# Seven raw weight slabs and six converted ones, in place of three and eight

## The chip, the cores and the metric

The kernel runs on one core of a Trainium2 chip. The metric is the device time of one execution in microseconds. The core has TensorE (PE, matrix products; weight loads are shown apart as PEld), VectorE (DVE), ScalarE (ACT), GpSimd (POOL) and SyncE (SP), which here issues nearly all the loads, and 16 DMA engines that all queues share.

## The reference

Two layers of a hybrid trunk over 256 tokens of 2048 features, float32. Each layer has a mixer and an MLP, with RMS norms ahead of and behind each:

```
for l in range(2):
    u = rmsnorm(h, g[0])
    proj = u @ w_in[l]                 # layer 0: 2048 x 6144, layer 1: 2048 x 7184
    # layer 0: gated short convolution, and chunked attention with a bias per head
    # layer 1: HGRN2 recurrence, and gated linear attention with a low-rank decay
    y = concat(heads) @ w_out[l]       # 2048 x 2048
    h = h + rmsnorm(y, g[1])
    u = rmsnorm(h, g[2])
    z = square(relu(u @ w1[l])) @ w2[l]    # 2048 x 8192, 8192 x 2048
    h = h + rmsnorm(z, g[3])
```

The weights are read from memory once each, some 400 MB in all.

## The kernel before

The 256 tokens are two tiles of 128 (t = 0 and 1). Every weight matrix is walked in blocks of 512 columns, and each block in slabs: one slab is 256 rows (SLAB = 2 groups of 128) by 512 columns, 512 KB. There are 784 of them.

**A slab's way.** `Block.load` does three things for each slab. SP loads it into a tile `raw` (pool `rawp`, RAW_BUFS buffers). ACT casts it to a high part `whi` in fp32r (L226). DVE subtracts that from the raw slab and so makes the low part `wlo` (L227). `whi` and `wlo` come from the pool `wp`, W_BUFS buffers of each. The raw buffer is free again when the subtraction is done; the pair is free when the last matmul on it is done. Products are made of the parts: high by high, high by low, low by high.

**Two kinds of blocks.** `Block.mm` puts the tokens on the partitions: for each token tile, six matmuls of 512 columns per slab (L240 to L242), with the sum of a block in one PSUM bank `acc`; so one slab is twelve matmuls. `UpBlock.mm` puts the weights' columns on the partitions and takes both token tiles at once: sixteen matmuls per slab, of 512 and 256 columns in turn (L275, L276), into four PSUM banks. At a block's end ACT and DVE empty the banks (`whole` L619, `relu` L453 and L476, and others).

**The order.** `run` (L316) walks the slabs of its blocks: load, hooks, matmuls of both token tiles. Every load of a slab is issued in that order on SP's queue, which also carries the loads of `h`, of `x` and of `norm_g` where a hook puts them. The program text gives priorities; a scheduler fixes, before the run, the order in which each engine gets its instructions, and may put a later matmul that is ready ahead of an earlier one that is not. On the chip each engine works strictly in that order.

**Three special places.** With `tail=4` the last four slabs of a run are walked for token tile 0 first, then for tile 1, so that the norm behind the product can begin for tile 0; the first of the four goes into a buffer of its own (`xhi`, `xlo`). With `lead` (the first run of each MLP) LEAD = 6 slabs are loaded and multiplied for token tile 0, then `lead()` makes the second tile's input (transposes on PE, L185, then `xt` on ACT, L176, and DVE, L178), then the six slabs are multiplied for tile 1. The second mixer begins right behind a run with a tail, so its first slabs too meet a second token tile whose input isn't there yet.

**Other users of raw buffers.** `prep_gla`, `prep_odd` and `load_bias` each take a buffer of `rawp` for a while.

In the second mixer `put_forget` transposes the forget gate `v` on PE, some slabs after its block has ended (`later`); `v` comes out of a chain of exponentials and products on ACT and DVE (L871 to L908).

Of the kernel before, what the change touches and what calls it, by code (L numbers as in the profile page):

```python
# [21 lines left out]
EPS = 1e-6  # L22
NT = 2
SLAB = 2
RAW_BUFS = 3
W_BUFS = 8
LEAD = 6
X_BUFS = 1
ACC_BUFS = 3
# [10 lines left out]
def trunk(ctx, tc, x, norm_g, e_win, rbf, e_wout, o_win, lbraw, smalls, wa2, ba, o_wout, w1, w2,  # L40
# [5 lines left out]
    x2p = ctx.enter_context(tc.tile_pool(name="x2p", bufs=8))  # L46
    rawp = ctx.enter_context(tc.tile_pool(name="rawp", bufs=RAW_BUFS))
    wp = ctx.enter_context(tc.tile_pool(name="wp", bufs=W_BUFS))
    st = ctx.enter_context(tc.tile_pool(name="st", bufs=4))
# [6 lines left out]

    nc.scalar.preload_act_table_set("natural_log_exp_and_others")

# [1 line left out]
    ident = const.tile([P, P], F32, name="ident")  # L60
    nc.scalar.dma_start(out=ident, in_=c_ident)
    ng_rows = const.tile([P, P], F32, name="ng_rows")
# [57 lines left out]
    def gcol(l, i):  # L120
        return ng_t[:, (l * 4 + i) * KT:(l * 4 + i + 1) * KT]

# [1 line left out]
    def rsqrt_of(ss, n, inv, base=None):  # L124
        """(ss * inv + EPS) ** -0.5; with base = (a, b, c, d): (ss * a + c) ** -0.5, where b = -a / 2, d = -c / 2."""
        a, b, c, d = base or (inv, -0.5 * inv, epst, -0.5 * EPS)
        hv = st.tile([P, n], F32, name="rs_v", bufs=4)
        nc.vector.tensor_scalar(out=hv, in0=ss, scalar1=b, scalar2=d, op0=ALU.mult, op1=ALU.add)
        r = st.tile([P, n], F32, name="rs_r", bufs=4)
        nc.scalar.activation(out=r, in_=ss, func=AF.Ln, scale=a, bias=c)  # L130
        nc.scalar.activation(out=r, in_=r, func=AF.Exp, scale=-0.5)
        a = st.tile([P, n], F32, name="rs_a", bufs=4)
        if n == 1:
            nc.vector.scalar_tensor_tensor(out=a, in0=r, scalar=hv, in1=r, op0=ALU.mult, op1=ALU.mult)
        else:
            nc.vector.tensor_tensor(out=a, in0=r, in1=r, op=ALU.mult)
            nc.vector.tensor_tensor(out=a, in0=a, in1=hv, op=ALU.mult)
        o = st.tile([P, n], F32, name="rs_o", bufs=12)
        nc.vector.scalar_tensor_tensor(out=o, in0=a, scalar=1.5, in1=r, op0=ALU.add, op1=ALU.mult)
        return o  # L140

    def powers(r):
        """Factors that stand in for the normalisation ahead of a squared ReLU."""
        r2 = st.tile([P, 1], F32, name="pw2")
        nc.vector.tensor_tensor(out=r2, in0=r, in1=r, op=ALU.mult)
        a, b = [st.tile([P, 1], F32, name="pw4" + n) for n in "ab"]
        nc.vector.tensor_scalar(out=a, in0=r2, scalar1=r2, scalar2=1.0 / D, op0=ALU.mult, op1=ALU.mult)
        nc.vector.tensor_scalar(out=b, in0=a, scalar1=-0.5, scalar2=None, op0=ALU.mult)
        return a, b, r2

    def base_of(ss, pre):
        """What rsqrt_of takes when but the last part of a sum of squares is there."""
        t = total(ss)
        c, d = [st.tile([P, 1], F32, name="base" + n) for n in "cd"]
        nc.vector.tensor_scalar(out=c, in0=t, scalar1=pre[0], scalar2=EPS, op0=ALU.mult, op1=ALU.add)
        nc.vector.tensor_scalar(out=d, in0=c, scalar1=-0.5, scalar2=None, op0=ALU.mult)
        return pre[0], pre[1], c, d

    def total(ss):
        t = st.tile([P, 1], F32, name="rs_t")  # L160
        nc.vector.tensor_reduce(out=t, in_=ss, axis=AX.X, op=ALU.add)
        return t
# [49 lines left out]
    class Block:  # L212
# [6 lines left out]
        def load(self, s, extra=None):  # L219
            k0 = self.kts[s * SLAB]  # L220
            raw = rawp.tile([P, SLAB, 512], F32, name="raw")
            nc.sync.dma_start(out=raw[:, :, 0:self.n], in_=self.wv[:, k0:k0 + SLAB, self.n0:self.n0 + self.n])
            pool, tag, bufs = (wp, "w", W_BUFS) if extra is None else (extra, "x", X_BUFS)
            hi = pool.tile([P, SLAB, 512], F32R, name=tag + "hi", bufs=bufs)
# [29 lines left out]
            return super().get(t, kt)  # L254

    class UpBlock(Block):
        """Columns of the weights on the partitions of the product, both token tiles at once."""

        def __init__(self, wv, n0, n, kts, lhs, evac, banks=None):
            super().__init__(wv, n0, n, kts, lhs, evac)  # L260
# [33 lines left out]
    soon = []  # L294

    def later(f, slabs=2):
        """f() that many slabs from now, so that what it puts on the tensor engine doesn't hold up the products."""
        soon.append([slabs, f])

    def tick(n=1):  # L300
# [50 lines left out]

    ALLK = list(range(KT))

# [1 line left out]
    def sumsq_of(src, jpool):  # L355
        ss = st.tile([P, 4], F32, name="ss4")
        for i in range(4):
            junk = jpool.tile([P, 512], F32, name="junk", bufs=1)
            nc.scalar.activation(out=junk, in_=src[:, i * 512:(i + 1) * 512], func=AF.Square,  # L359
                                 accum_out=ss[:, i:i + 1])  # L360
        return ss
# [27 lines left out]
            return f  # L389
        return t, [load(0), load(1)]  # L390

# [1 line left out]
    def out_proj(l, w, kts, X2, y, h, X, ypool, reload=()):  # L393
        gbc, gl = gbc_tile(ypool, l, 1)
        hooks = {2: gl[0:1], 5: gl[1:2]}
# [95 lines left out]
        run(down(NCH - 1), tail=TAIL, between=finish, extra=ypool)  # L491
        return lambda: finish(1)

# [1 line left out]
    hpool = tc.tile_pool(name="hpool", bufs=1)  # L495
    hp = hpool.__enter__()
    h = [hp.tile([P, D], F32, name=f"h{t}") for t in range(NT)]
# [17 lines left out]
    start = {i: [] for i in range(8)}  # L515
# [34 lines left out]
    yp_cm.__exit__(None, None, None)  # L550
    hpool.__exit__(None, None, None)

# [1 line left out]
    mixpool = tc.tile_pool(name="mix1", bufs=1)  # L554
    mp = mixpool.__enter__()
    X2 = XT()
# [31 lines left out]
def even_mixer(tc, nc, mp, st, aux, x2p, X, X2, rst, w, rbf, sm_t, flip, ident, Block, UpBlock, banks, pair, run,  # L588
# [5 lines left out]
    rbc = {}  # L594

    def spread_norms():
        """The norm factors of the tokens on every partition: as they are, for queries, and squared."""
        ones = mp.tile([P, P], F32, name="ones", bufs=1)
        nc.gpsimd.memset(ones, 1.0)
        ps = aux()  # L600
        for t in range(NT):
            diag = mp.tile([P, P], F32, name="part", bufs=2)
            nc.vector.tensor_scalar(out=diag, in0=ident, scalar1=rst[t], scalar2=None, op0=ALU.mult)
            nc.tensor.matmul(ps[:, t * P:(t + 1) * P], ones, diag, start=True, stop=True)
        for n in ("q", "k", "u"):
            rbc[n] = mp.tile([P, T], F32, name="rbc" + n, bufs=1)
        nc.scalar.copy(out=rbc["k"], in_=ps[:, 0:T])
        nc.scalar.activation(out=rbc["q"], in_=ps[:, 0:T], func=AF.Copy, scale=float(P) ** -0.5)
        nc.vector.tensor_tensor(out=rbc["u"], in0=rbc["k"], in1=rbc["k"], op=ALU.mult)

    def joined(ps, out, scale=None):
        """out = the two parts of a product of UpBlock, times scale."""
        a = mp.tile([P, T], F32, name="part", bufs=2)
        nc.scalar.copy(out=a, in_=ps[:, T:2 * T])
        if scale is None:
            nc.vector.tensor_tensor(out=out, in0=ps[:, 0:T], in1=a, op=ALU.add)
        else:
            z = mp.tile([P, T], F32, name="whole", bufs=2)
            nc.vector.tensor_tensor(out=z, in0=ps[:, 0:T], in1=a, op=ALU.add)  # L619
            nc.vector.tensor_tensor(out=out, in0=z, in1=scale, op=ALU.mult)  # L620
# [124 lines left out]
def odd_mixer(tc, nc, mp, st, aux, x2p, X, X2, rst, w, lbd, prep_gla, sm_t, ident, c_mask,  # L745
# [25 lines left out]
    def heads(a, t):  # L771
        return a.rearrange("p (h t n) -> p h t n", h=4, t=NT)[:, :, t, :]
# [4 lines left out]
    def feature_major(name, pool, bufs):  # L777
        return pool.tile([P, 4 * T], F32, name=name, bufs=bufs)

# [1 line left out]
    def scores(G):  # L781
        """G["K"], G["Q"]: keys and queries, features on the partitions, the queries times their own decay;
        G["B"]: the decay. Level w pairs the first half of each block of 2w tokens with its second half: the keys
        carry the decay up to the end of their half, the queries that from the start of theirs."""
        K, Q, B = G["K"], G["Q"], G["B"]
        sT = mp.tile([P, 8, P], F32, name="sT", bufs=1)
        nc.gpsimd.memset(sT, 0.0)
# [3 lines left out]
        for l, wd in enumerate(LEVELS):  # L791
            ps = aux()
            m = P - wd
            for u in range(8):
# [4 lines left out]
                                 start=True, stop=True)  # L799
            yield  # L800
            nc.vector.copy_predicated(
                out=sT[0:m].rearrange("p u (b two n) -> p u b two n", two=2, n=wd)[:, :, :, 1, :],
# [3 lines left out]
            if wd < 64:  # L806
# [10 lines left out]
                B = nxt  # L817
            else:
                bv = B.rearrange("p (h t two) -> p h t two", h=4, two=2)
                for a, t, i in ((K, 0, 1), (Q, 1, 0)):  # L820
                    half = heads(a, t).rearrange("p h (two n) -> p h two n", two=2)[:, :, 1 - i, :]
# [3 lines left out]
        for hd in range(4):  # L825
            nc.tensor.matmul(ps[:, hd * P:(hd + 1) * P], heads(K, 0)[:, hd, :], heads(Q, 1)[:, hd, :],
                             start=True, stop=True)
# [38 lines left out]
        X2.put(t, kg, split4(x2p, "x2", transpose4(z), sm_t[:, 24 + 4 * kg:28 + 4 * kg]))  # L866

    def neg_sigmoid(x, scale, o=None):
        """-sigmoid(-scale * x): a first reciprocal by exp and ln, then a Newton step."""
        d, r = tmp(), tmp()  # L870
        nc.scalar.activation(out=d, in_=x, func=AF.Exp, scale=scale)  # L871
        nc.vector.tensor_scalar(out=d, in0=d, scalar1=LN_MAX, scalar2=1.0, op0=ALU.min, op1=ALU.add)
        nc.scalar.activation(out=r, in_=d, func=AF.Ln)
        nc.scalar.activation(out=r, in_=r, func=AF.Exp, scale=-1.0)
        nc.vector.tensor_tensor(out=d, in0=d, in1=r, op=ALU.mult)
        o = r if o is None else o
        nc.vector.scalar_tensor_tensor(out=o, in0=d, scalar=2.0, in1=r, op0=ALU.subtract, op1=ALU.mult)
        return o
# [14 lines left out]
        return {"K": feature_major("x2", x2p, None), "Q": feature_major("x2", x2p, None),  # L893
                "B": feature_major("dec", mp, 1), "k": {}, "qk": {}, "v": {0: {}, 1: {}}}

# [1 line left out]
    def hgrn(g):  # L897
        lb = [mp.tile([P, 512], F32, name="gate", bufs=4) for _ in range(2)]
        lsrc = lbd.rearrange("i h d -> i (h d)")
# [34 lines left out]
                Block(wv, HI + g * 512, 512, ALLK, X.get, ev_i),  # L934
                Block(wv, HG + g * 512, 512, ALLK, X.get, ev_g)]

# [1 line left out]
    def gla():  # L938
        G = group()

# [62 lines left out]
    first, decay, rest = gla()  # L1003
# [46 lines left out]
```

## Time and profile before

| what | value |
|---|---|
| median of 3 runs | 2307.85 us (2306.0 to 2311.98) |
| span of the profiled execution | 2302.9 us |
| PE busy | 2276.5 us, 99% |
| PEld busy | 1920.3 us, 83% |
| DVE busy | 1412.6 us, 61% |
| ACT busy | 1093.6 us, 47% |
| DMA, mean over the span | 186 GB/s, the loads of slabs and x 56.2% of 16 engines' span |
| mean granted clock of PE | 0.997 |

The span runs from the first to the last instruction of one profiled execution; the time of a run has a little more around it. A view by time shows for each group of instructions its start, how long it took, its engine, its line in the kernel, what it writes and reads, and in brackets how long its engine stood idle before it and whose work ended that. A cast is ACT's L226, a subtraction DVE's L227.

### The profile page before, as it was taken

How to read it: one execution, taken by the hardware profiler on the slowest of the kernel's cores; microseconds unless marked ns; L12 is line 12 of the kernel's file. 1: busy time of each engine (PE TensorE's matmuls, PEld its weight loads, DVE VectorE, ACT ScalarE, POOL GpSimd, SP SyncE). 2: the span in 40 equal slices, each digit the busy share in tenths (PEclk: the TensorE clock that was granted, in tenths of full speed). 3: DMA queues.
4: the chain of work that ended last, by engine and by line, in shares of the span. 5: the costliest groups of instructions: out<-in, count | busy, mean ns of one | idle time of the engine just before them, and what ended most of it. 6: DMA issues, size and time to landing. Idle time of an engine off the chain costs nothing.

```text
span 2302.9 us, 30049 instructions
## 1 busy us (share of the span) xinstructions
PE 2276.5 (99%) x11518; PEld 1920.3 (83%) x11518; DVE 1412.6 (61%) x1873; ACT 1093.6 (47%) x1565; POOL 15.3 (1%) x30
## 2 busy tenths in 40 slices
PE   9999999999999999999999999999999999999998
PEld 7888888888888888888788888888888888888886
DVE  6656565755555555555777767657656555555555
ACT  6444445544444444444646454546444444444443
POOL 0000000000000000000000000000000000000000
PEclk9999999999999999999999999999999999999999
DMA  7564665655655556555554544565665655655653
GB/s 242 183 187 150 192 205 172 212 189 192 191 186 190 192 187 189 191 190 193 181 193 156 165 146 156 171 243 167 209 193 189 191 190 186 192 192 185 191 192 119
DMA packets 219231, 428.35 MB, mean 186 GB/s; under 512 B 13362, under 2 KB 14160, under 8 KB 218832
## 3 DMA queue, kind: packets, MB, share of 16 engines
q1 hardware_dynamic: 216992, 420.53, 56.2%
q0 software_dynamic: 1376, 4.79, 0.7%
q8 instruction: 90, 1.47, 0.2%
q10 hardware_dynamic: 720, 1.11, 0.1%
q14 instruction: 53, 0.43, 0.1%
HBM read 422.18 MB, written 4.20 MB: 185 GB/s over the span
## 4 chain that ended last, share of the span: by engine, by line
PE 87%; DMA 5%; DVE 4%; ACT 3%; issue 1%; DVEq 0%; ACTq 0%; POOLq 0%; SPq 0%
PE aux L275 20%; PE acc L240 17%; PE acc L242 17%; PE acc L241 17%; PE aux L276 10%; DMA raw<-e_win 2%; DVE wlo L227 2%; DMA raw<-w 2%; PE acc L275 2%; ACT whi L226 2%; PE aux L796 1%; PE aux L185 1%; PE acc L276 1%; ACT xt L176 1%; ACT junk L359 0%
## 5 line engine op out<-in xcount | busy, mean ns | idle before, releaser
L227 DVE TENSOR_TENSOR wlo<-raw,whi 128x1024 fp32r<-128x1024 f32 x780 | 953.7, 1224 | 785.2 <-ACT whi L226 783.5
L226 ACT CAST whi<-raw 128x1024 fp32r<-128x1024 f32 x780 | 821.5, 1054 | 1038.0 <-PE acc L242 509.8
L275 PE MATMUL aux<-xt,whi 128*128 128x512 f32 x2240 | 798.2, 398 | 1.5 <-DVE relu L453 1.5
L276 PE MATMUL aux<-xt,wlo 128*128 128x256 f32 x2240 | 628.4, 281 | 0.0
L275 PEld LDWEIGHTS aux<-xt,whi 128*128 128x128 f32 x2240 | 421.0, 188 | 105.8 <-DVE relu L453 2.1
L240 PE MATMUL acc<-whi,x 128*128 128x512 f32 x1264 | 493.2, 390 | 1.1 <-DVE relu L476 0.7
L242 PE MATMUL acc<-whi,x 128*128 128x512 f32 x1264 | 492.3, 389 | 0.0
L241 PE MATMUL acc<-wlo,x 128*128 128x512 f32 x1264 | 492.2, 389 | 0.0
L276 PEld LDWEIGHTS aux<-xt,wlo 128*128 128x128 f32 x2240 | 423.1, 189 | 0.5
L240 PEld LDWEIGHTS acc<-whi,x 128*128 128x128 f32 x1264 | 237.3, 188 | 51.0 <-DVE relu L476 1.1
L242 PEld LDWEIGHTS acc<-whi,x 128*128 128x128 f32 x1264 | 237.3, 188 | 49.8
L241 PEld LDWEIGHTS acc<-wlo,x 128*128 128x128 f32 x1264 | 237.3, 188 | 48.7
L240 PE MATMUL acc<-whi,xt 128*128 128x512 f32 x576 | 229.5, 399 | 0.3 <-ACT gate L882 0.3
L241 PE MATMUL acc<-wlo,xt 128*128 128x512 f32 x576 | 226.5, 393 | 0.0
L242 PE MATMUL acc<-whi,xt 128*128 128x512 f32 x576 | 226.0, 393 | 0.0
L242 PEld LDWEIGHTS acc<-whi,xt 128*128 128x128 f32 x576 | 108.7, 189 | 23.2 <-issue 0.3
L240 PEld LDWEIGHTS acc<-whi,xt 128*128 128x128 f32 x576 | 108.8, 189 | 22.4 <-ACT gate L882 0.7
L241 PEld LDWEIGHTS acc<-wlo,xt 128*128 128x128 f32 x576 | 108.9, 189 | 21.4
L275 PE MATMUL acc<-xt,whi 128*128 128x512 f32 x320 | 121.9, 403 | 3.8 <-DVE whole L619 3.8
L276 PE MATMUL acc<-xt,wlo 128*128 128x256 f32 x320 | 90.5, 283 | 0.0
L275 PEld LDWEIGHTS acc<-xt,whi 128*128 128x128 f32 x320 | 60.6, 189 | 18.8 <-DVE whole L619 4.4
L473 DVE TENSOR_TENSOR y<-acc,y 128x512 f32<-128x512 f32 x96 | 61.5, 682 | 0.0
(208 smaller groups left out, 1103.6 us busy)
## 6 DMA issues: line engine op xcount, KB each, us to landing
raw<-w SPq DMA_DIRECT2D x512, 512.0 KB, 3.6
raw<-o_win SPq DMA_DIRECT2D x112, 512.0 KB, 3.7
raw<-e_win SPq DMA_DIRECT2D x96, 512.0 KB, 4.2
raw<-e_wout SPq DMA_DIRECT2D x32, 512.0 KB, 4.3
raw<-o_wout SPq DMA_DIRECT2D x32, 512.0 KB, 3.9
gbc<-norm_g SPq DMA_DIRECT2D x8, 512.0 KB, 6.0
h<-x SPq DMA_DIRECT2D x8, 256.0 KB, 5.4
hsave<-h POOLq DMA_DIRECT2D x2, 1024.0 KB, 4.7
```

The source lines that it names most:

```text
L176: nc.scalar.activation(out=hi[:, k, :], in_=psv[:, k, :], func=AF.Copy, scale=g[:, k:k + 1])
L185: nc.tensor.transpose(out=ps[:, k * P:(k + 1) * P], in_=src[:, k * P:(k + 1) * P], identity=ident)
L226: nc.scalar.copy(out=hi[:, :, 0:self.n], in_=raw[:, :, 0:self.n])
L227: nc.vector.tensor_tensor(out=lo[:, :, 0:self.n], in0=raw[:, :, 0:self.n], in1=hi[:, :, 0:self.n], op=ALU.subtract)
L240: nc.tensor.matmul(ps, xh, hi[:, i, 0:self.n], start=first, stop=False)
L241: nc.tensor.matmul(ps, xh, lo[:, i, 0:self.n], start=False, stop=False)
L242: nc.tensor.matmul(ps, xl, hi[:, i, 0:self.n], start=False, stop=last)
L275: nc.tensor.matmul(self.ps[j], hi[:, i, cs], x, start=first, stop=False)
L276: nc.tensor.matmul(self.ps[j][:, 0:NT * P], lo[:, i, cs], x[:, 0, :], start=False, stop=last)
L473: nc.vector.tensor_tensor(out=y[t][:, cs], in0=ps, in1=y[t][:, cs], op=ALU.add)
L796: nc.tensor.matmul(ps[0:m, u * 64:(u + 1) * 64].rearrange("p (b n) -> p b n", n=wd), K[:, u * P:u * P + m], Q[:, us].rearrange("p (b two n ...
```

## The change

The same space in SBUF is shared out anew between the two pools: seven raw slabs can be in flight or waiting for their cast, where three could; six converted pairs can be held, where eight could. LEAD stays at 6. The rest of the diff takes out comments.

```diff
 NT = 2
 SLAB = 2
-RAW_BUFS = 3
-W_BUFS = 8
+RAW_BUFS = 7
+W_BUFS = 6
 LEAD = 6
 X_BUFS = 1
 ACC_BUFS = 3
```

## Rows read from the trace of the kernel before

**Rows 1.** Page, part 1: busy us, share of the span, instructions.

```profile
PE 2276.5 (99%) x11518; PEld 1920.3 (83%) x11518; DVE 1412.6 (61%) x1873; ACT 1093.6 (47%) x1565; POOL 15.3 (1%) x30
```

**Rows 2.** Timeline of ACT, 1068 to 1073 us: start, us, instruction, idle before.

```profile
1069.38 1.05 ACT L226 CAST whi<-raw 128x1024 fp32r<-128x1024 f32 x1 [1.66 <-PE acc L242]
1072.10 1.05 ACT L226 CAST whi<-raw 128x1024 fp32r<-128x1024 f32 x1 [1.67 <-PE acc L242]
```

**Rows 3.** Waits of PE: waiter, releaser, us in total, times, longest.

```profile
PE aux L185 <- issue: 4.6, 1, 4.6
PE acc L275 <- DVE whole L619: 3.8, 2, 2.0
PE aux L675 <- DVE pr L669: 1.9, 2, 1.5
...
PE aux L275 <- DVE relu L453: 1.5, 2, 1.0
...
PE acc L240 <- DVE relu L476: 0.7, 1, 0.7
PE aux L185 <- DVE gate L883: 0.6, 1, 0.6
PE acc L240 <- DVE whole L619: 0.4, 1, 0.4
```

**Rows 4.** Waits of ACT: the longest, and the longest on a load.

```profile
ACT whi L226 <- PE acc L242: 509.8, 326, 3.5
...
ACT whi L226 <- DMA raw<-e_win: 43.9, 30, 6.2
```

**Rows 5.** Timeline of ACT, DVE and PE, 58 to 61 us.

```profile
58.04 1.06 ACT L226 CAST whi<-raw 128x1024 fp32r<-128x1024 f32 x1 [0.32 <-DMA raw<-e_win]
...
59.13 1.23 DVE L227 TENSOR_TENSOR wlo<-raw,whi 128x1024 fp32r<-128x1024 f32 x1 [0.15 <-ACT whi L226]
60.27 0.42 DVE L619 TENSOR_TENSOR whole<-acc,part 128x256 f32<-128x256 f32 x1
...
60.74 0.50 PE L275 MATMUL acc<-xt,whi 128*128 128x512 f32 x1 [1.79 <-DVE whole L619]
```

**Rows 6.** Page, part 6: loads of slabs, KB each, median us to landing.

```profile
raw<-e_win SPq DMA_DIRECT2D x96, 512.0 KB, 4.2
```

**Rows 7.** Timeline of SP, ACT, DVE and PE, 1131 to 1149 us.

```profile
1131.92 0.37 SPq L222 DMA_DIRECT2D raw<-o_win  x1
...
1140.95 1.05 ACT L226 CAST whi<-raw 128x1024 fp32r<-128x1024 f32 x1 [4.45 <-DMA raw<-o_win]
...
1147.34 0.68 DVE L908 TENSOR_TENSOR v<-v,gate 128x512 f32<-128x512 f32 x1
...
1148.12 1.09 PE L185 MATMUL aux<-ident,v 128*128 128x128 f32 x4 [4.64 <-issue]
```

**Rows 8.** Busy us (instructions) by stretch: PE, PEld, DVE, ACT, POOL, clock, DMA share, GB/s.

```profile
62.20:65.70 3.50, 3.50 (x13) 3.02 (x12) 3.50 (x8) 1.72 (x4) 0.00 (x0) 0.51 0.76 243
65.70:72.00 6.30, 6.30 (x37) 5.46 (x37) 3.44 (x5) 2.83 (x4) 0.00 (x0) 1.00 0.69 216
...
1147.60:1151.10 3.50, 2.98 (x9) 2.58 (x10) 3.50 (x5) 2.19 (x5) 0.00 (x0) 0.51 0.48 148
```

**Rows 9.** Timeline of PE and ACT at the start of layer 0's MLP.

```profile
397.37 0.39 PE L240 MATMUL acc<-whi,xt 128*128 128x512 f32 x1
...
407.46 0.48 PE L242 MATMUL acc<-whi,xt 128*128 128x512 f32 x1
...
407.60 4.23 ACT L176 ACTIVATE xt<-aux,ng_t 128x128 fp32r<-128x128 f32 x16
...
412.22 1.16 ACT L226 CAST whi<-raw 128x1024 fp32r<-128x1024 f32 x1
```

**Rows 10.** Timeline of PE at the start of the second mixer.

```profile
1113.33 0.39 PE L240 MATMUL acc<-whi,xt 128*128 128x512 f32 x1
...
1123.00 0.48 PE L242 MATMUL acc<-whi,xt 128*128 128x512 f32 x1
```

## Prediction

> **What bounds the kernel now.** I read the page first for the share of each engine, then TensorE's own waits, then the waits of ACT, and then the order of time at each place where TensorE stood still.
>
> TensorE (PE) is busy 99% of the span and VectorE (DVE) 61% [rows 1]. A busy PE in this trace need not be a full one, but the starts agree with it: in the middle of a stage two casts that each wait for one slab of weights to be given back stand 2.72 us apart [rows 2], which is one slab of twelve 512-column matmuls at 0.227 us, with nothing between them. So a change of buffers can win only what PE loses, and that is little: 13.5 us in the waits of [rows 3], and what the clock takes after such a wait.
>
> No row of PE's waits names a weight tile (whi or wlo). The weights themselves are always there. What PE waits for is a PSUM bank to be emptied (whole, relu), or a tile that DVE makes for a transpose (pr, gate, v). The question is therefore why ACT and DVE, which are far from full, come late. ACT's waits answer: most of the time a cast waits for PE to give a converted slab back (509.8 us in 326 waits, harmless), but it also waits for raw slabs to land, 43.9 us for the first input projection alone [rows 4]. ACT and DVE work in order. A cast that waits for its DMA holds up the emptying of PSUM queued behind it.
>
> The stop at 60.74 us shows this whole [rows 5]: the cast at 58.04 waited for its DMA, the subtraction at 59.13 followed it, only then came "whole" at 60.27, and the matmul at 60.74 waited for that. The same order stands at the other wait for whole at L275, at the two for relu L453, at the one for relu L476 and at the one for whole at L240: 3.8 + 1.5 + 0.7 + 0.4 = 6.4 us.
>
> Why does the DMA come late? With three raw slots a load is issued when the subtraction three slabs back has ended. One turn of a slot is the landing, 4.2 us in the median of the first projection [rows 6], the cast 1.06 us and the subtraction 1.23 us [rows 5]: some 6.5 us for three slabs, 2.2 us each, against the 2.72 us that PE takes. That keeps up, but after any burst of other work on ACT or DVE it wins back only half a us per slab, and meanwhile each cast waits for its DMA.
>
> The longest wait, 4.6 us, is given as "issue", which says nothing. In order of time [rows 7] it is the same again: a raw slab issued at 1131.92 landed nine us later, while other loads filled the DMA engines; its cast stood 4.45 us at the head of ACT; the forget gate's exponentials were queued behind it; v was ready at 1148.0 and PE's transposes of v began at 1148.12.
>
> After two of these stops the clock fell. From 62.2 to 65.7 us the granted clock is 0.51 (the lower level, 1.2 GHz), and again from 1147.6 to 1151.1 [rows 8]. In the first, 13 matmuls took 3.5 us; at the rate of the row behind it (37 in 6.3 us) they take 2.2 us. So a fall costs 1.3 us, the two 2.6 us. PE had stood still for 2 us and for 5 us shortly before.
>
> **The change part by part.** No instruction is added or removed. In each partition a raw slab holds 4 KB and a converted one 8 KB (high and low part): 3 x 4 + 8 x 8 = 76 KB before, 7 x 4 + 6 x 8 = 76 KB after. Slabs ahead of PE: 11 before, 13 after.
>
> *Seven raw slabs.* A load is issued when the subtraction seven slabs back is done, so SP's queue runs four slabs (about 11 us) further ahead, and everything in that queue keeps its order, the loads of norm_g, of h and of x too. A slot held by prep_odd, prep_gla or load_bias is then one of seven, not of three. After a burst the raw slabs lie in SBUF and the casts follow one another at DVE's 1.23 us. If the transfers must be caught up too, 243 GB/s at a share of 0.76 [rows 8] make 1.6 to 2.2 us per slab, still under 2.72. So a cast waits for its DMA hardly ever after the first slabs. Terms:
> - the 6.4 us of bank waits: gone. Bounds 0 and 6.4; I take 6.4, since the one chain shown in full is the pattern of all.
> - the waits for pr and for gate, 1.9 + 0.6 = 2.5 us: a cast that waits for a DMA stands in these queues too, but beside much other work. Bounds 0 and 2.5; I take half, 1.3.
> - the 4.6 us at 1143: the slab of that cast is issued some 11 us earlier, before the crowd. The cast's wait of 4.45 us goes, and with it 4.4 us. Bounds 0 and 4.6.
> - the two falls of the clock: 2.6 us, bounds 0 and 2.6; I take 2.6, as the stops ahead of them go.
>
> Sum of gains: 6.4 + 1.3 + 4.4 + 2.6 = 14.7 us.
>
> *Six converted slabs.* In the steady state the cast of a slab waits for the matmuls six slabs back rather than eight. Weights are then ready 2 x 2.72 = 5.4 us later ahead of their use, of about 19 us (estimate: eight slabs of 2.72 us less a cast and a subtraction). Nobody waits for that.
>
> It costs where PE lives on the stock. At the start of an MLP, run() goes through LEAD = 6 slabs for token tile 0 while ACT and DVE still make the second tile's input. PE's row of acc<-whi,xt begins at 397.37 and goes on to 407.46 with 42 matmuls, only transposes between them: seven slabs of six matmuls for one token tile. The first input piece of tile 1 comes from the ACT block that begins at 407.60 [rows 9]. The seventh slab needs a seventh converted buffer, and with six there is none: its 6 x 0.227 = 1.36 us of work move behind the wait, and PE stands still that long. The MLP of layer 1 repeats the pattern. At the start of the second mixer it is again seven slabs for tile 0 before tile 1's input is there: 42 matmuls from 1113.33 to 1123.00 [rows 10]. Three times 1.36 = 4.1 us. Bounds: nothing below, as that work has no other place; above, see the second rival.
>
> The seventh slab can now be cast only when the first is given back, after both token tiles. ACT is free for it at 412.22 [rows 9]; its subtraction would end near 414.6, and PE needs it after six slabs of tile 1, near 417. The margin is 2.4 us, so I take nothing for it.
>
> Each of these three stops may bring the clock down. Bounds 0 and 3 x 1.3 = 3.9 us. Of the two waits for whole at L275, both near 2 us, one was followed by a fall and one not; the new ones are shorter. I take one in three, 1.3 us.
>
> The Trainium skill (TensorE: Matmul & The Clock Gate, section "HAM oscillation — how this bites in real kernels") speaks against the change here: a TensorE that is kept waiting again and again falls to its lower clock each time and pays for it in the matmuls that follow. The falls at 62.2 and 1147.6 agree; the other wait of 2 us does not. By that rule all three new stops would pay, and the time would be 2.6 us above mine.
>
> Sum: -14.7 + 4.1 + 1.3 = -9.3 us. The span of the profile is 2302.9 us and the median of the runs 2307.85 us, so 5 us lie outside the span, which the change doesn't touch. I take the sum from the median: 2307.85 - 9.3 = 2298.5 us. About 0.3% (6.9 us) can be told from no change, so "faster" begins below 2300.9 us.
>
> **Rivals.**
> 1. *The stop at 1143 stays.* The transposes of v stand at a fixed place in PE's queue, and v needs a chain of eight instructions on ACT and DVE; if the order of that chain comes out worse, the 4.4 us and one fall of the clock (1.3 us) are not won. For it: "issue" in the row names no releaser. Against: 4.45 of the 4.64 us are one DMA. -9.3 + 5.7 = -3.6 us: 2304.2 us, no change.
> 2. *Six buffers are too few at the three starts.* It decides if the seventh slab's cast comes more than 2.4 us later than I have it, because the input pieces, the sums of squares and the rsqrt stand ahead of it on ACT and DVE. Then PE stops a second time at each start, for up to one slab (2.72 us), and the clock falls each time (1.3 us): 3 x (1.36 + 2.72 + 1.3) = 16.1 us. With half of the gains (7.4 us) that is +8.7 us: 2316.6 us, slower.
> 3. *More slots don't bring more in flight*: SP's queue in order is held by another load, or by slots that are kept. The gains fall away and the 5.4 us stay: 2313.3 us, within 0.3%. Against it: SP's loads wait for raw slots (the subtraction) nearly everywhere.
>
> **How the numbers follow.** The forecast (2295 to 2301 us; all gains with no fall of the clock at the new stops give 2295) gets 0.57; rival 1, with the case that only some of the bank waits go, 0.28; rival 3 0.07; rival 2 0.08. Faster 0.56, same 0.36, slower 0.08. Range: from 2293 us, since PE's modelled ends hide a bit of each wait, up to 2309 us, which takes in rival 1 and leaves out most of rivals 2 and 3.
>
> **What would show it.** ACT's waits on raw loads fall from the rows of before to a few us outside the first 30 us. The waits for whole, relu and the "issue" row leave PE's list. New rows of about 1.4 us at L240 or L185 on xt or h appear at the two MLP starts and the second mixer's start, where the run of matmuls for tile 0 counts 36, not 42. I am wrong if PE's waits keep their sum with other names, or if a weight tile turns up among them.

## The result, and the profile after

The changed kernel takes 2287.09 us in the median (2285.99 to 2287.86, four runs) against 2307.26 us (2306.0 to 2311.98, four runs). The ratio is 0.9909, with a 95% interval of 0.9897 to 0.9921. That is 20.2 us less, where 9.3 were forecast. "Faster" came out as forecast; the time lies 6 us below the low end of the range (2293).

The page of the changed kernel: the span, part 1 (busy us, share of the span, instructions) and the first line of part 4 (shares of the chain that ended last).

```profile
span 2284.2 us, 30021 instructions
...
PE 2270.1 (99%) x11518; PEld 1918.1 (84%) x11518; DVE 1411.1 (62%) x1873; ACT 1093.9 (48%) x1565; POOL 15.3 (1%) x30
...
PE 97%; ACT 1%; DVE 1%; issue 0%; DMA 0%; DVEq 0%; ACTq 0%; POOLq 0%
```

The span is 18.7 us shorter, with the same number of instructions on each of these engines. PE's busy time fell by 6.4 us [rows 1] though it does the same work: part of what a stop costs stands in the trace as busy time, in matmuls at the lower clock and in ends that are modelled. The mean granted clock rose from 0.997 to 0.999.

The waits of PE in the changed kernel, the whole list (waiter, releaser, us in total, times, longest):

```profile
PE aux L73 <- DMA ng_rows<-norm_g: 1.7, 1, 1.7
PE aux L185 <- DVE h L379: 1.5, 4, 0.5
PE aux L514 <- DVE uT L709: 1.2, 1, 1.2
PE acc L241 <- DVE wlo L227: 0.4, 1, 0.4
```

Every row of [rows 3] is gone: whole, relu, pr, gate and "issue". The first and the third row stand in the first 7 us of the kernel, also before, and the change doesn't touch them. New are three of the four waits for h (the three starts) and one, of 0.4 us, for a weight tile.

The waits of ACT, the two longest and the only one of a cast into whi on a load:

```profile
ACT whi L226 <- PE acc L242: 582.9, 374, 4.1
ACT whi L226 <- PE aux L275: 438.2, 274, 2.2
...
ACT whi L226 <- DMA raw<-e_win: 2.5, 3, 1.7
```

Before, the casts waited 43.9 us for loads of e_win alone [rows 4]; now the casts into whi wait 2.5 us for all slabs together. What a cast waits for now is PE, and that is harmless.

The place of [rows 5], ACT and DVE in the changed kernel, 56 to 60 us (start, us, instruction, idle before):

```profile
56.08 0.42 DVE L619 TENSOR_TENSOR whole<-acc,part 128x256 f32<-128x256 f32 x1
...
56.85 1.05 ACT L226 CAST whi<-raw 128x1024 fp32r<-128x1024 f32 x1
...
59.39 1.05 ACT L226 CAST whi<-raw 128x1024 fp32r<-128x1024 f32 x1 [1.22 <-PE aux L275]
```

No cast waits for its DMA, "whole" isn't late, and PE goes on without a stop.

The place of [rows 7], SP, ACT, DVE and PE in the changed kernel, 1109 to 1133 us:

```profile
1109.14 0.37 SPq L222 DMA_DIRECT2D raw<-o_win  x1
...
1123.32 1.06 ACT L226 CAST whi<-raw 128x1024 fp32r<-128x1024 f32 x1 [0.51 <-PE acc L242]
...
1131.95 0.68 DVE L908 TENSOR_TENSOR v<-v,gate 128x512 f32<-128x512 f32 x1
...
1132.73 0.63 PE L185 MATMUL aux<-ident,v 128*128 128x128 f32 x4
```

The cast at 1123.32 is of the same slab (number 397, the first being 1) as the cast at 1140.95 of [rows 7]. Its load was issued at 1109.14, fourteen us ahead of its cast; before, nine. PE's transposes of v follow its matmuls with no idle time.

Where the time came from was measured by counting, in both traces, the slabs' matmuls that PE has begun, and comparing the time at which each count is reached. The lead of the changed kernel grows or shrinks at these places (one execution of each kernel; the kernel before varies from run to run by some us, so the single terms may too):

| place (time before) | lead, us | forecast |
|---|---|---|
| bank waits: 58 (2.1), 238 (2.2), 308 (0.7), 444 (0.8), 1089 (1.0), 1629 (1.2) | +8.1 | +6.4 |
| stop at 1143 | +4.8 | +4.4 |
| clock falls at 62 (1.6) and 1148 (1.2) | +2.8 | +2.6 |
| pr and gate: 85 to 110 (2.5), 1166 to 1180 (1.3) | +3.8 | +1.3 |
| pieces of under 1 us elsewhere | +2.1 | 0 |
| three starts (1.17, 0.69, 1.04) | -2.9 | -4.1 |
| new falls of the clock | 0 | -1.3 |
| sum | +18.7 | +9.3 |

The other 1.5 us of the 20.2 lie between the profiled executions and the medians. In all runs whose span is on record the time is 1.7 to 2.4 us above it, so of the 5 us that the prediction put outside the span some 3 us are that the profiled execution of the kernel before was a quick one.

### The profile page after: what moved, and what is told of

It reads as the page before. It is cut to its first block, busy times and chain, and to the rows that moved or that the text cites. A ratio compares the mean times of both kernels' runs of the same rounds, so it can differ in the third digit from the quotient of the medians.

```text
span 2284.2 us, 30021 instructions
## 1 busy us (share of the span) xinstructions
PE 2270.1 (99%) x11518; PEld 1918.1 (84%) x11518; DVE 1411.1 (62%) x1873; ACT 1093.9 (48%) x1565; POOL 15.3 (1%) x30
## 4 chain that ended last, share of the span: by engine, by line
PE 97%; ACT 1%; DVE 1%; issue 0%; DMA 0%; DVEq 0%; ACTq 0%; POOLq 0%
PE aux L275 23%; PE acc L240 18%; PE acc L242 18%; PE acc L241 18%; PE aux L276 12%; PE acc L275 3%; PE acc L276 2%; PE aux L796 1%; PE aux L185 1%; ACT xt L176 0%; ACT junk L359 0%; PE aux L843 0%; DVE wlo L227 0%; PE aux L681 0%; PE aux L657 0%
```

## The experiments

Two numbers were changed together, so the first question is which of them does it. The theory of the prediction, called the landing theory: only the raw slots bring the gain, as loads are issued earlier and casts no longer stand at the head of ACT's queue; the converted pairs cost at the three starts. The first rival, the order theory: another number of buffers makes the scheduler fix another order of work, and that order is what is better. The second question is what the stop at 1143 consisted of; the crowd theory says it was loads on GpSimd's queue beside the slabs' loads.

**Six pairs alone.** Three raw slots as before:

```diff
-W_BUFS = 8
+W_BUFS = 6
```

> The second half of the change alone: three raw slabs as before, six converted ones. Landing theory (the gain comes from the raw slots, since casts no longer stand in ACT's queue waiting for a load; the converted slots only cost work at three starts): the gain of 20.2 us is gone and the 2.9 us lost at the three starts stay, 2307.3 + 2.9 = 2310 us, with ACT's waits on raw loads near the 143 us of before. Order theory (the gain comes from the order in which the engines get their instructions, which differs from before in PE's list at 404 lines for the changed kernel and at 390 for this one, and only at 82 between these two): most of the gain is here too, about 2290 us. Depth theory (with fewer converted slots the casts run less far ahead and stand less in the way of the emptying of PSUM): 2295 us or less.

Measured: 2305.15 us (2301.29 to 2307.05), ratio 0.9982 (0.9973 to 0.9991); the kernel before took 2309.22 us on that chip. PE's longest waits in this kernel:

```profile
PE acc L275 <- DVE whole L619: 3.9, 2, 2.2
PE acc L240 <- ACT tmp L871: 2.6, 1, 2.6
```

ACT's waits on slabs' loads into whi in the same kernel:

```profile
ACT whi L226 <- DMA raw<-o_win: 45.7, 21, 5.9
ACT whi L226 <- DMA raw<-e_win: 29.7, 21, 6.1
ACT whi L226 <- DMA raw<-w: 28.5, 21, 1.9
ACT whi L226 <- DMA raw<-e_wout: 18.2, 9, 5.9
ACT whi L226 <- DMA raw<-o_wout: 9.2, 8, 1.5
```

The bank waits are back, and the casts wait 131.3 us for loads (143.5 before). The order theory falls: counted in the traces, position by position, PE's order of lines differs from that of the changed kernel at 21 of 11518 places, ACT's at 68 of 1565 and DVE's at 118 of 1873 (the kernel before differs from it at 201, 628 and 1143), and the gain is gone. The depth theory, which wanted 2295 us or less, falls too. The landing theory holds in the main, but not in the size: the three starts cost 1.1, 0.7 and 1.1 us, as they should, and yet the kernel came out 4 us faster than before, where 2.9 us slower was expected. In the profiled execution the fall of the clock at 62 is missing (1.6 us), and the stretches near 85 to 110 and 1629 and the start are shorter by 4 us in all.

**Seven pairs, three raw slots**, to see if fewer pairs help in themselves:

```diff
-W_BUFS = 8
+W_BUFS = 7
```

> Three raw slabs and seven converted ones, nothing else, between before (three and eight, 2307 to 2309 us) and the run with three and six (2305.2 us). If fewer converted slots shorten the refill after a burst (each cast waits for its load until the slots are full, and a slot less is a slab less to make good), the time lies between the two, near 2306 us, and ACT's waits on raw loads between 143 and 131 us. If the 4 us of the run with three and six came from the changed order alone, this run may lie outside, by up to 5 us on either side.

Measured: 2307.8 us (2302.56 to 2312.37), ratio 0.9996 (0.9984 to 1.0008). PE's longest waits in this kernel:

```profile
PE acc L275 <- DVE whole L619: 4.4, 2, 2.4
PE acc L240 <- ACT tmp L871: 3.5, 1, 3.5
PE aux L275 <- DVE relu L453: 3.3, 2, 1.8
PE acc L240 <- DVE relu L476: 2.3, 2, 1.4
```

Seven pairs give nothing, so fewer pairs don't help by degrees. The 4 us of the first experiment stay open: with three raw slots a run's time spreads over 3.5 to 10 us, and the traces of the five kernels with three slots differ in the stops that they have.

**Five raw slots and seven pairs**, which fill the same space (5 x 4 + 7 x 8 = 76 KB) and have the seventh pair that the starts want:

```diff
-RAW_BUFS = 3
-W_BUFS = 8
+RAW_BUFS = 5
+W_BUFS = 7
```

> Five raw slabs and seven converted ones, 76 KB as in the other two. Landing theory: one turn of a raw slot (landing 4.2, cast 1.06, subtraction 1.23 us) over five slots is 1.3 us per slab, DVE's own rate, so five are as good as seven; and the seventh converted slab gives back the six matmuls at each of the three starts: 2287.1 - 2.9 = 2284 us. Order theory says nothing definite, 2280 to 2300. Depth theory: slower than with six, by up to half of the difference between eight and six, about 2297 us.

Measured: 2289.26 us (2289.13 to 2289.42), ratio 0.9915 (0.9898 to 0.9931). At the three starts it wins 0.8, 0.7 and 0.9 us over the changed kernel, as expected; PE does 42 matmuls there again. It gives back 6.9 us at one place, 1124 to 1135 us. From the timeline of ACT and PE there:

```profile
1126.59 1.04 ACT L226 CAST whi<-raw 128x1024 fp32r<-128x1024 f32 x1 [5.36 <-DMA raw<-o_win]
1127.55 0.68 ACT L871 ACTIVATE tmp<-acc,nrst 128x512 f32<-128x512 f32 x1
...
1128.28 0.79 PE L240 MATMUL acc<-whi,xt 128*128 128x512 f32 x1 [3.85 <-ACT tmp L871]
```

The same stretch by engines (busy us and instructions of PE, PEld, DVE, ACT, POOL, then the granted clock, DMA share, GB/s):

```profile
1127.20:1134.20 7.00, 5.92 (x14) 4.66 (x15) 6.49 (x11) 5.90 (x9) 0.00 (x0) 0.51 0.92 332
```

It is the stop of [rows 7] again, in another dress: a cast that waits 5.4 us for its load, the emptying of a bank queued behind it, PE standing 3.85 us, and then seven us at the lower clock. The slab was issued at 1117.85, and GpSimd's two loads of the gate's bounds began at 1118.01.

**Four raw slots and seven pairs** (4 KB less in all):

```diff
-RAW_BUFS = 3
-W_BUFS = 8
+RAW_BUFS = 4
+W_BUFS = 7
```

> Four raw slabs and seven converted ones (72 KB). Landing theory: a turn of a slot over four slots is 1.6 us per slab against PE's 2.72, so a burst is made good at 1.1 us per slab where three slots win back 0.5; nearly all waits on loads go but the crowded stretch near 1140 us (a landing of nine us) may keep part of its 4.8 us: 2284 to 2290 us. If the number of slots in flight mattered in proportion, a fourth slot would give a quarter of the gain: 2302 us.

Measured: 2288.45 us (2287.77 to 2289.59), ratio 0.9911 (0.9897 to 0.9926). PE's longest wait in it:

```profile
PE acc L240 <- ACT tmp L871: 2.7, 1, 2.7
```

PE no longer waits for any whole, relu, pr or gate. One slot more than before is enough for all places but one.

**Four raw slots and six pairs**, so that only the raw slots differ from the changed kernel:

```diff
-RAW_BUFS = 3
-W_BUFS = 8
+RAW_BUFS = 4
+W_BUFS = 6
```

> One raw slab more than in the run with three and six, nothing else. Landing theory: a turn of a slot over four is 1.6 us per slab, so nearly all of the 18 us between three and seven slots come with the fourth, but for the crowd near 1130 us: 2287 to 2291 us. Proportion: a quarter of them, 2300 us. Order theory: anything between 2285 and 2310, without relation to the waits on loads.

Measured: 2292.27 us (2291.54 to 2293.55), ratio 0.9932 (0.9917 to 0.9946). Against the first experiment, which differs in the fourth slot alone, it wins 12.1 us: it is 16.2 us below the kernel before that ran beside it, and that one 4.1 us. Against the changed kernel it loses 5.6 us near 1130 to 1140. PE's longest waits in it:

```profile
PE aux L185 <- issue: 1.9, 1, 1.9
PE acc L240 <- ACT tmp L871: 1.7, 1, 1.7
```

So with six pairs the fourth slot brings some 12 us of the gain; the fifth to the seventh bring the rest, at this one place. With seven pairs the fourth slot alone brings more: 2288.45 us is 20.8 us below the kernel before that ran beside it, and 2307.8 us, with three slots, is level with its own. What makes the 9 us between 12 and 21 is open in part; the 4 us of three slots and six pairs are in it.

**Two raw slots**, eight pairs, to test the account of a slot's turn from the other side:

```diff
-RAW_BUFS = 3
+RAW_BUFS = 2
```

> Two raw slabs and the eight converted ones of before: the suspected loop made the bound. Landing theory: one slab per half a turn, (4.2 + 1.06 + 1.23) / 2 = 3.25 us, over PE's 2.72 us, for all 784 slabs: about 2548 us, 2480 to 2600, with PE now waiting for weights. Order and depth theory: the landing is hidden, under 2340 us.

Measured: 2573.27 us in one run. Two of PE's waits in it:

```profile
PE acc L241 <- DVE wlo L227: 41.6, 102, 2.3
...
PE aux L276 <- DVE wlo L227: 15.2, 48, 0.8
```

And the two longest of ACT on loads:

```profile
ACT whi L226 <- DMA raw<-w: 842.5, 455, 4.0
ACT whi L226 <- DMA raw<-o_win: 168.0, 84, 6.3
```

Now weights do turn up among PE's waits, and the loads set the pace: 2571.3 us of span for 784 slabs is 3.28 us each. The turn of a slot, by the medians of this kernel's page, is 3.6 to 3.8 us of landing, the cast 1.06 and the subtraction 1.23, so 5.9 to 6.1 us; over two slots 3.0 us, over three 2.0 us and over four 1.5 us, against the 2.72 us that PE takes. The 0.3 us between 3.0 and the measured 3.28 was not traced. Two slots can't keep up; three can in the middle of a stage, but not behind a burst.

**The kernel before, with two of the crowd's loads moved.** GpSimd's load of the mask goes to SP, sixteen slabs into the second mixer, and the small loads of wab go to SP's queue:

```diff
-            nc.gpsimd.dma_start(out=wab[16 * i:16 * i + 16, :], in_=wa2)
-        nc.gpsimd.dma_start(out=wab[32:33, :], in_=ba)
+            nc.sync.dma_start(out=wab[16 * i:16 * i + 16, :], in_=wa2)
+        nc.sync.dma_start(out=wab[32:33, :], in_=ba)
...
-    nc.gpsimd.dma_start(out=mask.bitcast(F32), in_=c_mask)
...
-    run(hgrn(0), rate=RATE)
+    run(hgrn(0), rate=RATE, hooks={16: [lambda: nc.sync.dma_start(out=mask.bitcast(F32), in_=c_mask)]})
```

> Three raw slabs and eight converted ones as before; only the loads of mask and of wab, which GpSimd issued at the second mixer's start, go through SP's queue instead, the mask behind the mixer's 16th slab, wab behind its 32nd. Crowd theory (the stop of 4.8 us at 1143 us and the fall of the clock behind it come from one raw load that shared the DMA engines with GpSimd's loads): the load of that slab lands in about 5 us instead of nine, and most of the 6.0 us lost there come back, the rest stays: 2302 to 2304 us. Chain theory (the stop comes from where v's exponentials and products stand in the queues of ACT and DVE): unchanged, 2307 us.

Measured: 2307.94 us (2303.91 to 2311.89), ratio 0.9996 (0.9987 to 1.0006): nothing. The "issue" row of PE shrank only from 4.6 to 3.3 us. The gate's two bounds, spread over the partitions by GpSimd's queue, still stand beside the slab. The two moves took little away: SP issued the mask at 1135.29 us in place of 1131.55, and the first load of wab at 1135.90 in place of 1134.10, while the late slab was still landing, until 1140.9.

**The same two moves with five raw slots and seven pairs:**

> The same two loads moved, with five raw slabs and seven converted ones. Without the move this share-out lost 5.6 + 1.3 us of PE's time near 1130 us in one stop and the fall of the clock behind it, and won 0.7 to 0.9 us at each of the three starts and 1.1 us at the first slab against seven and six. Crowd theory: the stop goes, 2289.3 - 6 = 2283.5 us, under the 2287.1 of seven and six. Chain theory: 2289 us again.

Measured: 2288.06 us (2287.47 to 2288.42), ratio 0.9912 (0.9898 to 0.9927). PE's wait at the bank fell from 3.9 to 2.6 us and the cast's from 5.4 to 4.1 us; 2.3 us at the place, not the whole stop.

**The same two moves with seven raw slots and six pairs:**

> The same two loads moved, with seven raw slabs and six converted ones. If seven slots are what carries this kernel over the crowd, moving the crowd wins nothing here: 2286 to 2288 us. If the two loads cost something by themselves on GpSimd's queue or on the DMA engines, this kernel gains the same few us as the other two.

Measured: 2287.02 us (2286.69 to 2287.08), ratio 0.9908 (0.9893 to 0.9923): no change from the changed kernel. Seven slots already carry PE over the crowd, so moving two of its loads is worth nothing there.

**The crowd taken away, four raw slots and seven pairs.** Both moves, and the first group's two bounds `lbk` are loaded behind the first mixer into buffers of their own:

```diff
+    lbk = [const.tile([P, 512], F32, name=f"lbk{i}") for i in range(2)]
...
+    for i in range(2):
+        nc.gpsimd.dma_start(out=lbk[i], in_=lbd.rearrange("i h d -> i (h d)")[i, 0:512].partition_broadcast(P))
...
-        lb = [mp.tile([P, 512], F32, name="gate", bufs=4) for _ in range(2)]
+        lb = lbk if g == 0 else [mp.tile([P, 512], F32, name="gate", bufs=4) for _ in range(2)]
...
-        for i in range(2):
+        for i in range(2 if g else 0):
```

> Four raw slabs, seven converted ones, and GpSimd's queue empty at the second mixer's start: mask and wab through SP's queue as in the runs before, and the forget gate's two bounds (512 KB with their spread over 128 partitions) loaded behind the first mixer into 4 KB of their own. Moving mask and wab alone took 2.3 of the 6.9 us off the stop with five slots and 1.8 of 6 with three. Crowd theory: the bounds' loads are the rest; the stop near 1130 us (3.9 + 0.7 us with four slots and seven converted) is gone, 2288.5 - 4.6 = 2284 us, under the 2287.1 of seven and six. Chain theory: the stop stays at over 2 us, 2287 us or more.

Measured: 2286.8 us (2285.34 to 2287.22), ratio 0.9907 (0.989 to 0.9923). PE's two waits that stood nearest to the place:

```profile
PE aux L186 <- issue: 0.9, 1, 0.9
PE acc L241 <- ACT v L928: 0.5, 1, 0.5
```

Against four slots and seven pairs with the crowd, PE gains 4.3 us at the place, and no clock falls. Between the two spans 2.1 us are left of that (2285.7 and 2283.6): 1.1 us come back right behind the place, up to 1182 us, 0.3 us at the start and 0.8 us behind the last slab's matmul. The time is 2.8 us above the 2284 that the crowd theory gave, but the stop is gone as it said. It ties with the changed kernel: four slots and seven pairs without the crowd are worth seven and six with it.

**The crowd taken away, three raw slots and seven pairs:**

> The same with three raw slabs. Crowd theory: of the 6.0 us that the stop at 1143 and its fall of the clock cost before, at least 4.5 are gone; the rest of the kernel keeps its waits on loads, so 2301 to 2304 us, and PE's wait given as issue goes under 1 us. Chain theory: the wait stays at 3 us or more and the time at 2306 us or more.

Measured: 2304.05 us (2301.41 to 2309.66), ratio 0.9983 (0.9974 to 0.9992). The "issue" row is 0.8 us, and PE stands 5.2 us better at the place than with three slots, seven pairs and the crowd; the whole gains 3.75 us. The crowd theory holds for the place; the bank waits stay, as expected. Mask and the first load of wab are still issued there (1132.06 and 1132.52 us, on SP's queue), and the slabs beside them land in 4.6 to 4.8 us. So of the crowd it is what went through GpSimd's queue, the bounds above all, that made the slab late; whether that lies in the queue or in the spreading of the bounds, no run tells apart.

Last, all thirteen kernels side by side (these eleven and the two of the case). Every one with three raw slots has rows for whole in PE's waits, and one or both of pr and gate. None with four, five or seven has a row for whole, relu, pr or gate. None of them beat the changed kernel by more than its spread. Four, five or seven raw slots with eight pairs would take 80 KB or more, against the 76 KB of both kernels; the gain without the cost at the starts wasn't tried in that form.

## Why the prediction was right in kind and wrong in size

**What bounds the kernel: right.** The waits of PE were the casts' waits for loads, passed on by engines that work in order. With the loads early, the waits on both lists go together, and with three slots they stay whatever the number of pairs.

**The bank waits: right, mis-sized.** 8.1 us for 6.4. The term was summed from the idle times of PE's list, and these are too small, in two ways that are alike at all six places. A matmul's end in the trace is modelled and covers the first 0.16 us of the stop. At 60.74 [rows 5] the last start ahead of the stop is 58.67, so 2.07 us lie between two starts that else are 0.12 us apart: 1.95 us lost, where the row says 1.79. The prediction named this for the low end of its range, but gave it only 2 us, on all the stops together. And behind each stop 0.34 us lie between the first matmul's start and the next, where it is 0.23 else. Over six places the difference is 1.7 us, 0.28 us each, which is these two. The figure from which that low end was taken is off as well: all gains at their upper bounds are 16.1 us, which with the 4.1 us at the starts gives 2295.9 us, not 2295.

**pr and gate: the step that failed.** The prediction halved these 2.5 us because much other work lies beside them. The two places gave 3.8 us in place of 1.3. At them PE's list of the kernel before has two more rows, which no term of the sum held:

```profile
PE acc L240 <- ACT gate L882: 0.3, 1, 0.3
PE aux L657 <- DVE kT L620: 0.3, 1, 0.3
```

All rows there make 3.1 us; the other 0.7 us has no row. In the changed kernel these two are gone too. The chain of the longer wait for pr (1.5 us, ended at 108.05) stood in the trace of the kernel before, ACT and DVE:

```profile
101.93 1.05 ACT L226 CAST whi<-raw 128x1024 fp32r<-128x1024 f32 x1 [2.89 <-DMA raw<-e_win]
...
107.22 0.69 DVE L669 TENSOR_TENSOR pr<-pr,rsum 128x512 f32<-128x512 f32 x1
```

In the changed kernel no cast there waits for a load. That pr and gate go together with the slots is shown by the kernels: one or both rows in all five with three slots, none in the seven with more. A wait on the same in-order engines, ahead of which casts wait for loads, belonged in the sum at full size; half of an unknown is no estimate. This is the largest of the terms that were off, 2.5 of 9.4 us, but with it right the forecast would still have been 2296 us.

**The stop at 1143: right.** 4.8 us for 4.4. Rival 1 falls: the chain of v came in time. Its cause is the two things together that [rows 7] suggested, a slot that is free late and a crowd of other loads; seven slots remove it with the crowd in place, four and five do not (2.7 and 3.9 us of PE's wait stay), and without the crowd four do. In the loads of 1115 to 1145 us of the kernel before (queue, operation, count, KB each, median us from issue to landing) the crowd stands as

```profile
raw<-o_win SPq DMA_DIRECT2D x7, 512.0 KB, 3.7
hsave<-h POOLq DMA_DIRECT2D x1, 1024.0 KB, 4.4
gate<-lbd POOLq DMA_DIRECT2D x2, 256.0 KB, 7.4
mask<-c_mask POOLq DMA_DIRECT2D x1, 224.0 KB, 5.2
```

and in the changed kernel, which is some 11 us ahead there, over the same times,

```profile
raw<-o_win SPq DMA_DIRECT2D x13, 512.0 KB, 7.8
...
gate<-lbd POOLq DMA_DIRECT2D x2, 256.0 KB, 6.9
```

There are 13 slabs in place of 7, landing in 7.8 us in the median in place of 3.7, and no cast there waits for them: more slots didn't make loads faster, they made slow ones harmless.

**The clock.** The two old falls gave 2.8 us for 2.6. Three windows of the changed kernel, over the work at which [rows 8] has the first fall (59.1 to 61.2 us in this trace) and the second (from 1132 us on), with the same columns:

```profile
54.00:60.00 6.00, 6.00 (x36) 5.30 (x35) 4.92 (x10) 3.74 (x7) 0.00 (x0) 1.00 0.58 179
60.00:66.00 6.00, 6.00 (x37) 5.30 (x36) 2.74 (x3) 2.56 (x3) 0.00 (x0) 1.00 0.66 186
1132.00:1138.00 6.00, 6.00 (x31) 4.63 (x30) 5.50 (x8) 3.90 (x7) 0.00 (x0) 1.00 0.93 328
```

Between 9.3 us and the last 5 us of the span the changed kernel has no fall, so the 1.3 us charged for a new one didn't come. The prediction weighed the Trainium skill there (TensorE: Matmul & The Clock Gate, section "HAM oscillation — how this bites in real kernels") and read it as a price on all three new stops, 3.9 us; measured is 0. The reading was the prediction's own: the section tells of a TensorE that waits for a DMA ahead of every step of its product, not of three lone stops hundreds of us apart. The run nearest to that case is the one with two raw slots, in whose list PE waits 238 times: its granted clock fell twelve times between 125 and 1777 us, so that trace agrees that many waits bring falls, and not that each one does.

**Six pairs: right in place, too dear.** Three new waits stand where the prediction put them, and PE does 36 matmuls for tile 0 instead of 42 at each. The start of layer 0's MLP in the changed kernel, PE and ACT (compare [rows 9]):

```profile
387.40 0.39 PE L240 MATMUL acc<-whi,xt 128*128 128x512 f32 x1
...
395.33 0.39 PE L242 MATMUL acc<-whi,xt 128*128 128x512 f32 x1
396.15 1.23 PE L185 MATMUL aux<-ident,h 128*128 128x128 f32 x8 [0.43 <-DVE h L379]
...
396.82 4.23 ACT L176 ACTIVATE xt<-aux,ng_t 128x128 fp32r<-128x128 f32 x16
...
401.44 1.16 ACT L226 CAST whi<-raw 128x1024 fp32r<-128x1024 f32 x1
```

The run of matmuls on xt for tile 0 begins at 387.40, and the first xt of tile 1 at 396.82: 9.42 us later. Before it was 10.23 us, from 397.37 to 407.60 [rows 9]. The other two starts have it 0.7 us earlier. The prediction moved the seventh slab's matmuls behind the wait but left the wait's end where it was, although the seventh cast and subtraction left ACT's and DVE's queues too; that this is why the input comes earlier is argued, not shown. Net the starts cost 2.9 us for 4.1, though the earlier input alone would make it 1.9 (4.1 less 2.2); the 1.0 us between was not followed up, but 0.4 us of it is the one weight row in PE's list. It stands at the second mixer, and it is not the seventh slab but the sixth: with eight pairs that was cast at 1108.43, ahead of the run's first matmul at 1113.33 [rows 10]; with six it was cast at 1104.39, 2.9 us behind the first matmul, and its subtraction ended at 1109.08. The margin of 2.4 us for the seventh slab held at all three, as PE's list has no other row for a weight tile. By its letter this row is one of the signs by which the prediction called itself wrong; it is 0.4 us, and the account doesn't hang on it.

**The sum.** The lines of the table that were mis-sized, against the forecast: bank waits 1.7, pr and gate 2.5, starts 1.2, clock 1.3 + 0.2, stop 0.4, and 2.1 us at places that no row of PE's list names. All of them err to the same side. The range's low end, 5.5 us under the forecast, was therefore too high by 6. Rivals 2 and 3 both fall: no second stop came at the starts beyond that 0.4 us, and the waits of the casts into whi on loads fell from 143.5 to 2.5 us.

## What to carry to other kernels

Count a slot's turn (landing, cast, subtraction) against the time the consumer takes for its share, and then try one slot more; here the turn of some 6 us fits three slots of 2.72 us each in steady state, and the fourth brought most of the gain. Where slow loads come in a row, as near 1130 us, five slots still stopped PE and seven did not. A waiting load costs through what is queued behind it on an in-order engine, so look for late PSUM emptying and not only for waits on the weights. Sum stops from start to start on the engine that bounds, not from the idle time in a list, and charge every wait with the same cause in full.

## What the runs showed that was not expected

**Spread as a sign.** Kernels with three raw slots spread by 3.5 to 10 us from run to run (10 to 19 runs each; the kernel before 2305.65 to 2311.64 over 19 runs), those with four or more by at most 2 us, over four runs each. That it is the landings that vary, and that with more slots a late one doesn't reach PE, is argued from this, not shown.

**The clock after a stop.** A fall followed a stop of 2 us near 60 us in the kernel before, and none followed one of the same size at 238, yet with three slots and seven pairs there was one at 240. In the twelve kernels with three or more slots none followed a stop of up to 0.9 us. A fall cost 1.2 to 1.6 us where it lasted 3.4 us; with five slots, behind the stop of 3.85 us, the lower clock lasted 6.8 us.

**Loads that share a place.** Two loads of 256 KB that GpSimd's queue spreads over the partitions took 6.9 to 7.4 us, and the slab's load issued in the same us took 8.7 us with five slots (1117.85 to its cast at 1126.59), against 3.7 us in the median. With four slots and seven pairs the casts' longest wait for a load of o_win was 4.6 us beside them and 1.7 us without.
